# Token-order products with 512 weight columns at a time, and PSUM banks handled one token tile at a time

## The chip, the cores and the metric

The kernel runs on one core of a Trainium2 chip. The metric is device time in microseconds for one execution, as the median of several runs. The engines are named as the profile names them: PE (matrix products) with PEld (loading of the stationary operand), DVE, ACT, POOL, and SP, which issues most DMAs. Products land in PSUM, in tiles of 128x512 fp32 that are called banks here; DVE and ACT read them out.

## The reference

The program computes a two-layer trunk on 512 tokens of width 1024, all in fp32. Cut to what matters here:

```
for l in range(2):
    h = rmsnorm(x, norm_mix_g[l])
    a_q, a_k, a_v, a_gk, a_g, b_z, b_xbc, b_dt, c_q, c_k, c_v, gates = split(h @ w_in[l])
    y_gla  = gla_mixer(a_q, a_k, a_v, a_gk, a_g, ...)     # 4 heads, key 128, value 256, causal chunks
    y_ssm  = ssd_mixer(b_z, b_xbc, b_dt, ...)              # 4 groups of 8 heads
    y_diff = diff_mixer(c_q, c_k, c_v, positions, ...)     # 8 heads, two softmaxes of 64 each, value 128
    mixed  = sigmoid gates * (y_gla @ w_br_gla, y_ssm @ w_br_ssm, y_diff @ w_br_diff), summed
    x = x + mixed @ w_out[l]
    x = x + square(relu(rmsnorm(x) @ w_mlp_up[l])) @ w_mlp_down[l]
return rmsnorm(x)
```

`h @ w_in[l]` has 14,384 columns. Ten slices of 512 columns of it per layer matter here: `a_v` and `a_g` (GLA, 1024 columns each) and `c_q`, `c_k`, `c_v` (differential attention, 1024 columns each).

## The kernel before, in words

Every fp32 value that goes through a large product is split into a high part and a rest (both in the type fp32r), and a product is three: high times high, high times rest, rest times high. The activations stay in SBUF as pairs of `hl` tiles with the model dimension in the partitions. The weights come by DMA as blocks of 512 KB (`wraw`, 2 buffers); half a block at a time is split by ACT (`whi`) and by DVE or POOL (`wlo`), 4 buffers each. `Weight.split` (L511) does that.

There are two kinds of large ("dense") products. Most are in feature order: 128 weight columns are the stationary operand and 512 tokens stream, and the result takes one PSUM bank with features in the partitions (`item_a`, L848; `item_a2` does two such results, L876). The second kind is in token order, `item_b` (L924): 128 tokens of the activations are the stationary operand and **256 weight columns** stream, so that the result has tokens in its partitions. One item covers 256 columns and all 512 tokens: four token tiles share two banks, half a bank each. It takes both banks when it starts, runs 8 k-steps of 12 products of 128x256, and hands both to `fin` when the last one is issued. There are 20 such items per layer: GLA v and g for 4 heads (`gla_head`, `vg_item`, L1311), and q, k, v for 4 pairs of differential heads (`diff_pair`, `nat_item`, L1579).

PSUM has 4 banks under the name `d` for dense results and 4 under the name `m` for the small products of the mixers. A `d` bank is given back when its last reader is done: for v a copy by ACT and a subtraction by DVE (`z`, `tw`), for g a Tanh by ACT and a multiplication by DVE (`z`), for q, k, v of the attention one ACT copy.

The order of everything is made when the program is built. `Flow.run` keeps a clock of its own and a list of mixer tasks (Python generators, which yield what they wait for: an `Event`, or room in a pool) and of dense items. It issues a task's next step when what that waits for should be there, and otherwise a piece of the dense item that is running; another dense item is begun only when the running one has ended. The other engines' instructions are recorded by `Timed` and let out in order of their planned start (`Model.post`). So each engine has one fixed queue, and on the chip each instruction waits for the semaphores of what it needs: if DVE is later than planned, PE stands still at the first instruction that needs it, with everything behind.

Names: `z` (in the order listings `z4`) are tiles for gated and natural-order results, pool size 5; `tw` are tiles of the SSD decay weights and the v rests, pool size 3; `pj`, `tt`, `g1`, `hl` are further tiles of the mixers. `cth` is a two-buffer ring for scratch.

The two lines that take and fill a token-order result:

```
o = it.held[t // 2].ap[:, (t % 2) * 256:(t % 2) * 256 + 256]
f.mm(o, ah[:, ts], wh[:, j], k == 0 and t % 2 == 0, False)
```

The layer's items stand in this order in the list: SSD groups 0 to 3 (B, C, four X, four Z each, with the branch products `w_br_ssm` of the group before), then per GLA head K, Q, V, G with the last `w_br_ssm` after head 0 and eight gate items after head 1, then q, k, v of the four pairs, then gates, `w_br_gla`, `w_br_diff`, `w_out` and the MLP. The planner looks 16 items ahead and may take a later one.

## Time and profile before

| what | value |
|---|---|
| median of 3 runs | 2842.09 us (2841.82 to 2842.11) |
| span of the profiled execution, first to last instruction | 2836.2 us |
| PE busy in it | 2744.4 us, 97% |
| DVE busy | 1847.2 us, 65% |
| ACT busy | 1239.0 us, 44% |
| POOL busy | 774.7 us, 27% |
| mean granted clock of PE | 0.985 |

The page gives the profiled execution by its span; the median of the runs stands 5.9 us above that, which is what lies around the first and last instruction. The busy time of PE counts matmuls to the end of their way through the array, with overlap, so it says where PE stood still (the gaps) and not how long one product holds it; that is read from the distance between the starts of products that follow each other.

### The profile page before, as it was taken

To read this page: it belongs to the slowest core of one execution; us is meant where nothing else is said; L and a number is where in the kernel's file an instruction comes from. 1 tells how busy PE (TensorE), PEld (TensorE's weight loads), DVE (VectorE), ACT (ScalarE), POOL (GpSimd) and SP (SyncE) were. 2 spreads that over 40 slices of the span, in tenths; PEclk is the share of its full clock that TensorE was granted. 3 is DMA by queue.
4 is the path that set the end of the run, shared out by engine and by line. 5 is a ranking of instruction groups with operands and counts; after the bars stand their busy time and mean duration, and the time that the engine had idled before them with its cause. 6 is when DMAs were issued, how large, how long until landed. Compare 5 with 4: busy or idle time off the path is not lost.

```text
span 2836.2 us, 44502 instructions
## 1 busy us (share of the span) xinstructions
PE 2744.4 (97%) x16908; PEld 2349.9 (83%) x16908; DVE 1847.2 (65%) x3848; ACT 1239.0 (44%) x2381; POOL 774.7 (27%) x821
## 2 busy tenths in 40 slices
PE   7799999999999999999998999989999999999998
PEld 5678788899998888888866778878999988888887
DVE  7797878757777355444487888785666754654445
ACT  4355445545655333223344444454556543432222
POOL 4555454313232001001036343452223210011001
PEclk9899999999999999999999999999999999999999
DMA  4334432332222343333335343323222223333332
GB/s 133 92 107 110 113 112 76 85 86 78 69 68 75 97 126 94 96 95 100 95 95 138 93 119 101 110 61 94 81 81 63 75 82 102 116 100 98 96 98 83
DMA packets 458226, 268.97 MB, mean 95 GB/s; under 512 B 19014, under 2 KB 450748, under 8 KB 458012
## 3 DMA queue, kind: packets, MB, share of 16 engines
q1 hardware_dynamic: 457396, 265.07, 33.5%
q8 instruction: 133, 2.18, 0.3%
q10 hardware_dynamic: 616, 1.06, 0.1%
q14 instruction: 81, 0.66, 0.1%
HBM read 259.60 MB, written 6.49 MB: 94 GB/s over the span
## 4 chain that ended last, share of the span: by engine, by line
PE 82%; DVE 9%; POOL 2%; DMA 2%; issue 2%; ACT 2%; SPq 1%; DVEq 0%; ACTq 0%; POOLq 0%
PE d L353 73%; PE m L353 7%; PE m L357 2%; DVE tt L79 2%; DVE wlo L79 2%; DVE pj L79 1%; POOL tw L79 1%; DMA tw<-acs 1%; DVE g L79 1%; SPq L79 1%; DVE hl L79 1%; DVE z L79 1%; DMA wraw<-in_w_in 0%; ACT tt L79 0%; ACT whi L79 0%
## 5 line engine op out<-in xcount | busy, mean ns | idle before, releaser
L353 PE MATMUL d<-hl,whi 128*128 128x512 f32 (+2 forms) x5696 | 1779.3, 394 | 32.8 <-DVE tt L79 13.4
L353 PEld LDWEIGHTS d<-hl,whi 128*128 128x128 f32 (+1 forms) x5696 | 1059.5, 189 | 250.3 <-issue 24.4
L353 PE MATMUL d<-hl,wlo 128*128 128x512 f32 (+2 forms) x2848 | 1114.2, 391 | 7.9 <-DVE wlo L79 7.3
L79 ACT ACTIVATE whi<-wraw 128x512 fp32r<-128x512 f32 (+1 forms) x868 | 544.1, 628 | 1099.0 <-PE d L353 954.3
L79 DVE TENSOR_TENSOR wlo<-wraw,whi 128x512 fp32r<-128x512 f32 (+1 forms) x762 | 578.5, 762 | 483.8 <-ACT whi L79 477.7
L353 PEld LDWEIGHTS d<-hl,wlo 128*128 128x128 f32 (+1 forms) x2848 | 537.7, 189 | 123.7 <-DVE wlo L79 8.5
L353 PE MATMUL d<-whi,hl 128*128 128x256 f32 x2560 | 482.0, 289 | 0.0
L353 PEld LDWEIGHTS d<-whi,hl 128*128 128x128 f32 x2560 | 401.8, 193 | 2.9
L353 PE MATMUL d<-wlo,hl 128*128 128x256 f32 x1280 | 363.5, 284 | 0.0
L79 POOL TENSOR_TENSOR wlo<-wraw,whi 128x512 fp32r<-128x512 f32 x106 | 147.1, 1390 | 725.7 <-ACT whi L79 451.1
L79 POOL TENSOR_TENSOR tt<-tt 128x512 f32<-128x512 f32 (+1 forms) x132 | 151.6, 1158 | 625.9 <-ACT hl L79 530.2
L353 PEld LDWEIGHTS d<-wlo,hl 128*128 128x128 f32 x1280 | 246.3, 192 | 0.0
L79 DVE TENSOR_TENSOR res<-res,d 128x512 f32<-128x512 f32 (+1 forms) x130 | 86.7, 676 | 135.7 <-PE d L353 133.8
L79 POOL TENSOR_SCALAR tw<-tw,acn 128x128 f32<-128x128 f32 x101 | 92.1, 927 | 70.4 <-DMA tw<-acs 61.6
L79 ACT ACTIVATE tt<-tt 128x256 f32<-128x256 f32 (+3 forms) x190 | 87.6, 502 | 30.8 <-DMA tt<-acs 14.0
L79 DVE SCALAR_TENSOR_TENSOR pj<-d,cols,pj 128x511 f32<-128x511 f32 (+2 forms) x120 | 88.7, 743 | 1.5 <-ACT pj L79 0.3
L79 POOL TENSOR_TENSOR tw<-tw,tt 128x1024 f32<-128x1024 f32 x32 | 82.2, 2579 | 14.5 <-ACT tw L79 14.2
L79 ACT ACTIVATE tt<-m 128x512 f32<-128x512 f32 (+6 forms) x133 | 59.3, 451 | 54.7 <-PE m L353 34.2
L79 ACT ACTIVATE pj<-m 64x256 fp32r<-64x256 f32 (+1 forms) x160 | 66.7, 421 | 35.9 <-PE m L357 21.4
L353 PE MATMUL m<-z,tt 128*128 128x128 f32 (+1 forms) x432 | 75.2, 284 | 3.1 <-DVE g L79 1.7
L79 ACT ACTIVATE tw<-m,mx 128x384 f32<-128x384 f32 (+3 forms) x128 | 66.8, 524 | 25.4 <-DVE mx L79 24.3
L79 DVE SCALAR_TENSOR_TENSOR tt<-d,tt 128x512 f32<-128x512 f32 x64 | 44.0, 690 | 51.3 <-PE d L353 49.9
(179 smaller groups left out, 2621.9 us busy)
## 6 DMA issues: line engine op xcount, KB each, us to landing
wraw<-in_w_in SPq DMA_DIRECT2D x224, 512.0 KB
wraw<-in_w_mlp_up SPq DMA_DIRECT2D x64, 512.0 KB
wraw<-in_w_mlp_down SPq DMA_DIRECT2D x64, 512.0 KB
tw<-acs SPq DMA_DIRECT2D x32, 512.0 KB
wraw<-in_w_br_ssm SPq DMA_DIRECT2D x32, 512.0 KB
wraw<-in_w_br_gla SPq DMA_DIRECT2D x16, 512.0 KB
wraw<-in_w_br_diff SPq DMA_DIRECT2D x16, 512.0 KB
wraw<-in_w_out SPq DMA_DIRECT2D x16, 512.0 KB
```

What stands on the lines that cost most here:

```text
L79: fn = lambda a=args, k=kw: real(*a, **k)
L353: self.model.post(self.clock - c, lambda: self.nc.tensor.matmul(out, lhsT, rhs, start=start, stop=stop))
L357: self.model.post(self.clock - 0.109, lambda: self.nc.tensor.transpose(out, in_, ident))
```

## The change

`item_b` is replaced by `item_w`. One item now covers 512 columns of weights: a weight half-block is 128 rows of the model dimension by 512 columns (before: 256 rows by 256 columns), a k-step is 12 products of 128x512, and there are 8 half-blocks. Each of the four token tiles has a bank of its own. The bank for tile t is taken just before that tile's first products, and after the last k-step `fin` is called for each tile as soon as its products are issued, so banks go back one at a time. Per layer there are 10 such items in place of 20.

So that 512 columns belong together, the mixers work on more heads at a time: `gla_duo` has the V and G items of two heads in common and lists K, Q of both heads ahead of them; `diff_duo` has q, k, v of four heads (before: two). The results are cut into `z` tiles by token pairs instead of by head, the v rests move from `tw` to `z`, and the pool `z4` has 8 tiles instead of 5. `rope` works on two token tiles and eight half-heads instead of four and four: as many elements and calls as before. In the listing of the layer the last `w_br_ssm` items and the eight gate items both come after the first GLA duo. `rs_y` has 6 buffers instead of 2, and `dynamic_dma_scratch_size=1024` reserves less SBUF, which makes room for the larger pool; SP and ACT issue the DMAs as before.

```
-    def item_b(self, w, c0, acts, fin, extra=(), cond=()):
+    def item_w(self, w, c0, acts, fin, extra=(), cond=()):
         def body(it, i, wt):
-            wh, wl = wt
-            for j in range(2):
-                k = i * 2 + j
-                ...
-                for t in range(NT):
-                    o = it.held[t // 2].ap[:, (t % 2) * 256:(t % 2) * 256 + 256]
-                    ts = slice(t * P, (t + 1) * P)
-                    f.mm(o, ah[:, ts], wh[:, j], k == 0 and t % 2 == 0, False)
-                    f.mm(o, al[:, ts], wh[:, j], False, False)
-                    f.mm(o, ah[:, ts], wl[:, j], False, k == KT - 1 and t % 2 == 1)
-        blocks = [b for h in range(2) for b in Block(self, [w[h * 512:(h + 1) * 512, c0:c0 + 256]], 4, 256).parts()]
-        return self.item(blocks, [("d", ([P, 512],))] * 2 + list(extra), body, fin, acts, cond, False)
+            wh, wl = [v[:, 0] for v in wt]
+            ...
+            for t in range(NT):
+                if i == 0:
+                    yield {"d": 1}
+                    it.banks.append(self.T("d"))
+                else:
+                    yield None
+                o = it.banks[t].ap
+                ts = slice(t * P, (t + 1) * P)
+                f.mm(o, ah[:, ts], wh, i == 0, False)
+                f.mm(o, al[:, ts], wh, False, False)
+                f.mm(o, ah[:, ts], wl, False, i == KT - 1)
+                if i == KT - 1:
+                    fin(it, t, it.banks[t])
+        blocks = [b for k in range(0, KT, 2)
+                  for b in Block(self, [w[k * P:(k + 2) * P, c0:c0 + S]], 2, S).parts()]
+        return self.item(blocks, list(extra), body, lambda it: None, acts, cond, False)
...
+    def gla_duo(self, l, duo, h, slot, evy):
+        ...
+        for hd in (2 * duo, 2 * duo + 1):
+            self.gla_head(l, hd, h, shared, slot, evy[hd])
+        ...
+            def fin(it, t, ps):
+                x = it.held[t // 2].ap[:, t % 2]
+                if gate:
+                    self.act(x, ps.ap, AF.Tanh, scale=0.5)
+                    V.scalar_tensor_tensor(x, x, 1.0, ps.ap, op0=ALU.add, op1=ALU.mult)
+                    ...
+                else:
+                    self.split(x, it.held[2 + t // 2].ap[:, t % 2], ps.ap)
+                ps.free()
...
+        vg_item(O_V + duo * 512, False)
+        vg_item(O_G + duo * 512, True)
...
+    def diff_duo(self, l, duo, h, slot, evy):
...
+            def fin(it, t, ps):
+                x = it.held[t // 2]
+                self.act(x.ap[:, t % 2], ps.ap, AF.Copy)
+                ps.free()
+                if t % 2 and i < 2:
+                    self.rope(x.ap, t - 1)
...
-        for hd in range(4):
-            self.gla_head(l, hd, h, gs[hd // 2], evg[hd])
-            if hd == 0:
+        for duo in range(2):
+            self.gla_duo(l, duo, h, gs[duo], evg)
+            if duo == 0:
                 self.ssm_part(l, 3, evy[3], quads, merged, evm[3])
-            if hd == 1:
                 self.ssm_gates(l, h, merged, evm[3], gated)
-        for pr in range(4):
-            self.diff_pair(l, pr, h, ds[pr // 2], evd[pr // 2])
+        for duo in range(2):
+            self.diff_duo(l, duo, h, ds[duo], evd[duo])
```

The order on the engines changes with it. First place: PE in layer 0 where the first V item begins, behind the last Z item of the SSD mixer (`d_3270` before, `d_3310` after). Each name is one bank's worth of result. Before:

```order
L353 MATMUL d_3270<-hl_371,wlo_3233 128x512
L353 MATMUL d_3326<-whi_3268,hl_369 128x256
L353 MATMUL d_3326<-whi_3268,hl_370 128x256
L353 MATMUL d_3326<-wlo_3269,hl_369 128x256
L353 MATMUL d_3326<-whi_3268,hl_369 128x256
L353 MATMUL d_3326<-whi_3268,hl_370 128x256
L353 MATMUL d_3326<-wlo_3269,hl_369 128x256
L353 MATMUL d_3327<-whi_3268,hl_369 128x256
```

After:

```order
L353 MATMUL d_3310<-hl_371,wlo_3273 128x512
L353 MATMUL d_3366<-whi_3308,hl_369 128x512
L353 MATMUL d_3366<-whi_3308,hl_370 128x512
L353 MATMUL d_3366<-wlo_3309,hl_369 128x512
L353 MATMUL d_3373<-whi_3308,hl_369 128x512
L353 MATMUL d_3373<-whi_3308,hl_370 128x512
L353 MATMUL d_3373<-wlo_3309,hl_369 128x512
L353 MATMUL d_3382<-whi_3308,hl_369 128x512
L353 MATMUL d_3382<-whi_3308,hl_370 128x512
L353 MATMUL d_3382<-wlo_3309,hl_369 128x512
L353 MATMUL d_3444<-whi_3308,hl_369 128x512
```

Two banks carried the whole V item; now the first k-step alone goes into four, the fourth (`d_3444`) after nine products.

The same place on DVE. `z4_...<-z4_...,d_...` is the last read of a Z item's bank; the `pj` and `hl` rows between belong to the end of SSD group 2, the `wlo` rows split weights. Before:

```order
L79 SCALAR_TENSOR_TENSOR pj_2389<-pj_2389,cols0_92,tt_3240 128x512
L79 TENSOR_TENSOR wlo_3405<-wraw_3300,whi_3404 128x512
L79 TENSOR_TENSOR hl_3278<-pj_2389,hl_3277 128x512
L79 TENSOR_TENSOR wlo_3439<-wraw_3352,whi_3438 128x512
L79 SCALAR_TENSOR_TENSOR z4_3071<-z4_3071,d_3270 128x512
L79 TENSOR_TENSOR wlo_3472<-wraw_3352,whi_3471 128x512
L79 TENSOR_TENSOR tw_3135<-d_3326,z4_3134 128x512
L79 TENSOR_TENSOR tw_3135<-d_3327,z4_3134 128x512
```

After:

```order
L79 SCALAR_TENSOR_TENSOR z4_2311<-z4_2311,d_3246 128x512
L79 TENSOR_TENSOR wlo_3365<-wraw_3274,whi_3364 128x512
L79 SCALAR_TENSOR_TENSOR pj_2161<-pj_2161,cols0_92,tt_3280 128x512
L79 TENSOR_TENSOR hl_3318<-pj_2161,hl_3317 128x512
L79 SCALAR_TENSOR_TENSOR pj_2207<-pj_2207,cols0_92,tt_3280 128x512
L79 SCALAR_TENSOR_TENSOR pj_2251<-pj_2251,cols0_92,tt_3280 128x512
L79 TENSOR_TENSOR hl_3318<-pj_2207,hl_3317 128x512
L79 TENSOR_TENSOR hl_3318<-pj_2251,hl_3317 128x512
L79 SCALAR_TENSOR_TENSOR pj_2428<-pj_2428,cols0_92,tt_3280 128x512
L79 TENSOR_TENSOR wlo_3448<-wraw_3274,whi_3447 128x512
L79 TENSOR_TENSOR hl_3318<-pj_2428,hl_3317 128x512
L79 SCALAR_TENSOR_TENSOR z4_2376<-z4_2376,d_3310 128x512
```

In both orders the last Z item's bank is read out at the end of that chain; before, the V item's own banks follow it and nothing on PE needed that bank earlier.

Second place: DVE in layer 1, again where the first V item begins (the Z items' banks are `d_16884`, `d_16948` before and `d_15926`, `d_15991` after). Before:

```order
L79 SCALAR_TENSOR_TENSOR z4_16703<-z4_16703,d_16884 128x512
L79 SCALAR_TENSOR_TENSOR pj_15846<-pj_15846,cols1_93,tt_16917 128x512
L79 TENSOR_TENSOR wlo_17000<-wraw_16911,whi_16999 128x512
L79 TENSOR_TENSOR hl_16945<-pj_15846,hl_16944 128x512
L79 SCALAR_TENSOR_TENSOR z4_16764<-z4_16764,d_16948 128x512
```

After:

```order
L79 TENSOR_SCALAR tw_15934<-tw_15934,acn_13540 128x128 x6
L79 SCALAR_TENSOR_TENSOR z4_15743<-z4_15743,d_15926 128x512
L79 SCALAR_TENSOR_TENSOR pj_14886<-pj_14886,cols1_93,tt_15960 128x512
L79 TENSOR_TENSOR wlo_16043<-wraw_15954,whi_16042 128x512
L79 SCALAR_TENSOR_TENSOR z4_15804<-z4_15804,d_15991 128x512
```

Six `tw` rows of a third SSD chunk moved ahead of the two reads, and the `hl` row moved behind the second.

## Rows read from the trace of the kernel before

**Rows 1.** The page, part 1 and a line of part 2 (tenths busy, 40 slices)

```profile
PE 2744.4 (97%) x16908; PEld 2349.9 (83%) x16908; DVE 1847.2 (65%) x3848; ACT 1239.0 (44%) x2381; POOL 774.7 (27%) x821
...
PE   7799999999999999999998999989999999999998
```

**Rows 2.** Waits of PE over the span: total us, times, longest

```profile
PE m L353 <- DVE tt L79: 14.6, 12, 3.5
...
PE d L353 <- DVE pj L79: 11.8, 2, 8.8
```

**Rows 3.** Groups by form: busy us, mean ns of one | idle before

```profile
L353 PE MATMUL d<-whi,hl 128*128 128x256 f32 x2560 | 482.0, 289 | 0.0
...
L353 PE MATMUL d<-wlo,hl 128*128 128x256 f32 x1280 | 363.5, 284 | 0.0
```

**Rows 4.** Chain that ended last: start us, us, what, products

```profile
692.34 8.63 PE d L353 x72
...
1089.96 339.64 PE d L353 x1497
```

**Rows 5.** PE timeline, end of a Z item and start of V, layer 0

```profile
365.14 0.39 PE L353 MATMUL d<-hl,wlo 128*128 128x512 f32 x1
365.37 0.40 PE L353 MATMUL d<-whi,hl 128*128 128x256 f32 x2
```

**Rows 6.** DVE timeline at the same place

```profile
367.11 0.68 DVE L79 SCALAR_TENSOR_TENSOR z<-z,d 128x512 f32<-128x512 f32 x1
367.70 0.74 DVE L79 SCALAR_TENSOR_TENSOR pj<-pj,cols,tt 128x512 f32<-128x512 f32 x1
368.88 2.48 DVE L79 TENSOR_TENSOR wlo<-wraw,whi 128x512 fp32r<-128x512 f32 x1 [0.43 <-ACT whi L79]
...
377.85 0.68 DVE L79 SCALAR_TENSOR_TENSOR z<-z,d 128x512 f32<-128x512 f32 x1
```

**Rows 7.** PE timeline, start of the first V item of layer 1

```profile
1753.06 0.40 PE L353 MATMUL d<-whi,hl 128*128 128x256 f32 x2
```

**Rows 8.** DVE timeline at the same place

```profile
1753.99 0.68 DVE L79 SCALAR_TENSOR_TENSOR z<-z,d 128x512 f32<-128x512 f32 x1
...
1758.18 1.77 DVE L79 TENSOR_TENSOR hl<-pj,hl 128x512 fp32r<-128x512 f32 x1
1759.88 0.68 DVE L79 SCALAR_TENSOR_TENSOR z<-z,d 128x512 f32<-128x512 f32 x1
```

**Rows 9.** PE timeline, the longest wait in GLA of layer 0

```profile
469.62 0.66 PE L353 MATMUL m<-tt 128*32 128x32 f32 x32 [4.01 <-DVE sd L79]
```

**Rows 10.** Stretches: busy us of each engine, then PE's granted clock, DMA

```profile
440.00:520.00 80.00, 73.19 (x721) 63.74 (x720) 71.42 (x155) 45.45 (x101) 42.13 (x34) 0.94 0.24 71
469.60:476.00 6.40, 6.38 (x151) 6.05 (x152) 5.81 (x14) 1.56 (x5) 3.52 (x3) 0.59 0.25 84
680.00:760.00 80.00, 80.00 (x661) 79.20 (x660) 55.55 (x151) 49.60 (x121) 22.13 (x38) 1.00 0.26 73
1683.00:1690.00 7.00, 6.97 (x39) 5.58 (x39) 5.57 (x9) 2.79 (x5) 1.84 (x2) 0.76 0.63 188
1825.00:1905.00 80.00, 71.53 (x765) 61.55 (x764) 69.56 (x152) 44.99 (x100) 36.71 (x31) 0.94 0.24 71
```

**Rows 11.** PE timeline, last products of a G item

```profile
613.15 0.28 PE L353 MATMUL d<-wlo,hl 128*128 128x256 f32 x1
```

**Rows 12.** DVE timeline: that G item's two banks read out

```profile
614.63 1.28 DVE L79 SCALAR_TENSOR_TENSOR z<-z,d 128x512 f32<-128x512 f32 x2
```

**Rows 13.** PE timeline, last product of an attention item

```profile
696.36 0.28 PE L353 MATMUL d<-wlo,hl 128*128 128x256 f32 x1
```

**Rows 14.** ACT timeline: that item's two banks read out

```profile
698.08 0.60 ACT L79 ACTIVATE z<-d 128x512 f32<-128x512 f32 x1
...
700.94 0.60 ACT L79 ACTIVATE z<-d 128x512 f32<-128x512 f32 x1
```

More of the change, by code (lines that the diff above doesn't have):

```diff
@@ L963, in rsqrt_small @@
         v = pool.tile([P, n], F32, name="rs_v", bufs=2)
-        y = pool.tile([P, n], F32, name="rs_y", bufs=2)
+        y = pool.tile([P, n], F32, name="rs_y", bufs=6)
         t = pool.tile([P, n], F32, name="rs_t", bufs=2)
@@ L1309, in gla_head @@
         qk_item(O_Q + hd * P, "q", st["evq"], P ** -0.5)
-        def vg_item(c0, key, ev, gate):
-            def fin(it):
-                x = it.held[2]
-                for i in range(2):
-                    ps = it.held[i]
-                    pv = ps.ap.rearrange("p (t c) -> p t c", c=256)
-                    xv = x.ap[:, 2 * i:2 * i + 2]
-                    if gate:
-                        self.act(xv, pv, AF.Tanh, scale=0.5)
-                        V.scalar_tensor_tensor(xv, xv, 1.0, pv, op0=ALU.add, op1=ALU.mult)
-                        G.tensor_tensor(xv, xv, self.gnr.unsqueeze(1).broadcast_to([P, 2, 256]), op=ALU.mult)
-                        ps.free()
-                    else:
-                        self.split(xv, it.held[3].ap[:, 2 * i:2 * i + 2], pv)
-                        ps.free()
-                st[key] = x if gate else it.held[2:]
-                ev.t = f.at(*[x.ap for x in it.held[2:]])
-            self.item_b(w, c0, h, fin, extra=[("z4", ([P, NT, 256],))] if gate else
-                        [("z4", ([P, NT, 256], F32R)), ("tw", ([P, NT, 256], F32R))])
-        vg_item(O_V + hd * 256, "v", st["evv"], False)
-        vg_item(O_G + hd * 256, "g", st["evg"], True)
         def gates():
@@ L1503, in scores @@
             qe.free()
-            for x in parts + st["v"]:
+            for x in parts + shared["v"]:
                 x.free()
@@ L1533, in finish @@
             if done[0] == NT:
-                st["g"].free()
+                for x in shared["g"]:
+                    x.free()
                 evy.t = f.at(*[q.ap[:, m0:m0 + 2] for q in slot[0]])
@@ L1556, in diff_lambda, with rope @@
         nc.vector.tensor_scalar(self.dcol, self.cols[l][:, C_DN:C_DN + 1], 1.0 - li, None, op0=ALU.mult)
-    def rope(self, x):
+    def rope(self, x, t0):
         G = self.nc.gpsimd
@@ L1576, in diff_pair @@
         nat, evs = [None] * 3, [Event() for _ in range(3)]
-        left = [2]
+        left = [4]
         half = (slice(0, 64), slice(64, P))
         def nat_item(i, off):
-            def fin(it):
-                x = it.held[2]
-                for j in range(2):
-                    self.act(x.ap[:, 2 * j:2 * j + 2], it.held[j].ap.rearrange("p (t c) -> p t c", c=256), AF.Copy)
-                    it.held[j].free()
-                if i < 2:
-                    self.rope(x.ap)
-                nat[i] = x
-                evs[i].t = f.at(x.ap)
-            self.item_b(w, off + pr * 256, h, fin, extra=[("z4", ([P, NT, 256],))])
+            def fin(it, t, ps):
[4 more added lines that the diff above has]
+                    self.rope(x.ap, t - 1)
+                if t == NT - 1:
+                    for b in it.held:
+                        b.users = 1 if i == 2 else 4
+                    nat[i] = it.held
+                    evs[i].t = f.at(*[b.ap for b in it.held])
+            self.item_w(w, off + duo * S, h, fin, extra=[("z4", ([P, 2, S],))] * 2)
         for i, off in enumerate((O_CQ, O_CK, O_CV)):
             nat_item(i, off)
+        nat_of = lambda i, t, hh: nat[i][t // 2].ap[:, t % 2, hh * P:(hh + 1) * P]
         def head(hh):
-            hd = pr * 2 + hh
             def turn(i, t0, n):
@@ L1598, in turn @@
                 for t in range(n):
-                    f.tr(tp.ap[:, t * P:(t + 1) * P], nat[i].ap[:, t0 + t, hh * P:(hh + 1) * P], self.ident)
-                if hh == 1 and t0 + n == NT:
-                    nat[i].free()
+                    f.tr(tp.ap[:, t * P:(t + 1) * P], nat_of(i, t0 + t, hh), self.ident)
+                for b in nat[i][t0 // 2:(t0 + n) // 2]:
+                    b.free()
                 return tp
@@ L1700, in step @@
             if left[0] == 0:
-                nat[2].free()
+                for b in nat[2]:
+                    b.free()
             V.tensor_scalar(o.ap[:, t], op.ap[:, :P], rc[:, t, 0:1], None, op0=ALU.mult)
@@ L1704, in step @@
             ev.t = f.at(o.ap[:, t])
-        for hh in range(2):
+        for hh in range(4):
             f.spawn(head(hh))
```

51 lines of the change are left out of this document (35 added, 16 removed).

## The prediction, made before the change was run

> **What bounds the kernel now.** I read the page's busy times first, then who makes PE wait, then the stretches. PE is busy 2744.4 of 2836.2 us, and the slices show it near full from the third of 40 on [rows 1]. The reader is to see two things: PE is the bound wherever it stands at 9, and the 92 us without it lie in a few places where PE waits for DVE [rows 2]. In the attention part PE is busy 80.00 of 80 us; in the GLA part it is 73.19 of 80 in layer 0 and 71.53 of 80 in layer 1, with DVE busy 71.42 and 69.56 of the same 80 [rows 10]. So in the first place time saved on PE is time saved, in the second DVE sets the pace, and a saving on PE may only become more waiting.
>
> **What the wider products save.** The 3840 narrow products (2560 and 1280) [rows 3] run in 40 items. Their spacing is read from the chain: 72 of them in 8.63 us, 119.9 ns each; 1497 products of 512 columns take 339.64 us, 226.9 ns each [rows 4]. Two narrow ones cost 239.8 ns, one wide one 226.9, so 12.9 ns go for each pair. 3840 / 2 = 1920 pairs give 1920 x 12.9 ns = **24.7 us less on PE**. All else that items do is equal in number: bytes of weights, weight splits (half as many items, twice as many halves), read-outs of 128x512, `rope` and gate multiplications. I cost those at nothing; they lie beside PE's work and their count per microsecond of PE hardly moves. The larger `z4` pool lets some Z items of SSD groups 2 and 3 in layer 0 go earlier; layer 1 keeps its order up to the first V item. I cost that at nothing too, with 3 us to either side.
>
> Here the Trainium skill speaks against the change. Its page "TensorE: Matmul & The Clock Gate", section "Back-to-back issue gap", gives for products alone a spacing of N/2.4 ns plus 2.5 ns at full clock, which would leave 2.5 ns a pair, an estimated 4.8 us in all. The trace's 119.9 and 226.9 ns do not agree with it: both are about 13 ns over their columns.
>
> **What four banks cost: the first V item.** An item took two of the four `d` banks; now it takes all four within its first nine products, 9 x 0.2269 = 2.04 us. Whatever item came last must be read out by then, or PE stands, and with it every mixer product and weight behind it in PE's queue.
>
> Layer 0. Before, the first V item starts at 365.37, right behind a Z item [rows 5]. That Z item's bank is read last by the DVE multiplication at 377.85, which ends at 378.53 [rows 6]: DVE has the end of SSD group 2 in front of it. Nobody on PE waited, since V had two other banks. In the new order the fourth bank is that of the last Z item, and the same chain stands ahead of its read-out: from one `z` row to the next the old order takes 367.11 to 378.53 = 11.42 us [rows 6], with four weight splits in it; the new one has two, so 11.42 - 2 x 0.68 = 10.1 us. It begins 367.11 - 365.37 = 1.74 us after the V item's start, or up to 1.7 us later, since six `tw` rows (some 0.28 each) stand ahead. So the bank is free 11.8 to 13.5 us after the start and wanted after 2.04: PE waits 9.8 to 11.5 us. If the one stretched row (2.48 us for a split, where 0.68 is usual) is ordinary this time, it is 1.8 less, 8.0. I take **10 us**.
>
> Layer 1. V starts at 1753.06 [rows 7], the two Z read-outs begin at 1753.99 and 1759.88 [rows 8], the second ends at 1760.56, 7.50 us after the start. In the new order the `hl` row of 1.77 us stands behind it, and six `tw` rows (1.7 us) ahead: 5.7 to 7.4 us, less 2.04 = 3.7 to 5.4. I take **4.5 us**.
>
> A long wait has a second price. After the 4.01 us wait [rows 9] the granted clock of the next 6.4 us is 0.59, so part of them ran at 1.2 instead of 2.4 GHz: 6.4 x 0.41 = 2.6 us lost; behind the wait of 11.8 - 8.8 = 3.0 us in layer 1 [rows 2] it is 7.0 x 0.24 = 1.7 us [rows 10]. I add 2.6 and 1.7.
>
> **What four banks cost elsewhere.** Other places per layer where a wide item starts or ends tight: the first G item, the two-bank `w_br_ssm` products after it, the second G item, the first attention item right behind it, and the first and second items of the second attention duo. Ten to twelve in all; I count 11. A bank is given back 2.04 us before the same tile of a following wide item needs it. A G item's two banks are read out by 614.63 + 1.28 = 615.91, its last product began at 613.15 [rows 11, 12]: about 2.5 us after its end, 0.5 us over the cover. In attention, where ACT is full of exponentials, the second bank is free at 700.94 + 0.60 = 701.54, some 4.9 us after the end of the product begun at 696.36 [rows 13, 14], 2.9 us over. An item between, or small products of the tasks, cover all of it. Between 0 and 2.9 a place I take 0.5, nearest to the G row: 11 x 0.5 = **5.5 us**, with 0 and 15 as ends. Where a bank is late, nothing new is waiting on DVE or ACT; their queues only drain.
>
> **The GLA part.** Two heads' score stages now run in the same stretch, under one G item and four `w_br_ssm` items, where before they came one after the other. PE's idle time there is 80 - 73.19 = 6.8 and 80 - 71.53 = 8.5 us [rows 10], because DVE is late. The DVE work is the same, denser at first and thinner behind. I carry over the 15.3 us unchanged: 0 in the sum, -8 and +20 as bounds.
>
> The Trainium skill, "Trainium Kernel Development and Optimization", section "Best Practices", says that tiling for TensorE speeds up compute but not the evacuation of PSUM. The rows on the banks above agree with it.
>
> **Sum**, on the profiled span of 2836.2 us: -24.7 + 10 + 2.6 + 4.5 + 1.7 + 5.5 + 0 = -0.4 us. The runs stand 5.9 us over the span, which nothing here touches, so the time is 2842.1 - 0.4 = 2841.7; I say **2841 us**.
>
> **The rivals.**
> Faster: DVE is less late. The waits at V take their low ends (8.0 and 3.7, less clock loss, 3), the others 1, and PE's standing early lets DVE catch up, so half of the 15.3 us in GLA goes: -24.7 + 8 + 3.7 + 3 + 1 - 7.6 = -16.6, **2825 us**. For it: in attention PE never waits and DVE is busy only 55.55 of 80 [rows 10]. Against it: the chain of rows 6 does not depend on PE, and between V and GLA lie 70 us in which DVE would recover anyway.
> Slower: DVE cannot carry two GLA heads at once. If PE's idle time there doubles (+15.3) the sum is +14.9, **2857 us**. It decides where the two heads' stretch has over 12 us of PE idle a layer; from there the change loses. For it: DVE is already at 89% of such a stretch. Against it: the stretch behind is thin, and PE's products of the other head can fill.
> The change doesn't do what it says: the 13 ns are not a price per product but something that wide products with moving weights keep. Then nothing is saved and the waits stay: +24.3, **2866 us**. Against it: the spacing of rows 4 is constant over 1497 products. By the skill's formula above, read as such a case, it would be 2842.1 - 4.8 + 24.3, an estimated 2862 us.
>
> **How the numbers follow.** The forecast (own range 2834 to 2848) has 0.38, the faster rival 0.34, the slower one 0.24, no saving 0.04. About 0.2%, 5.7 us, is what a measurement of this kernel can tell from no change. Of the forecast's share 0.34 lie within that and 0.02 on either side: faster 0.36, same 0.34, slower 0.30. The range of 8 in 10 reaches from the faster rival to the slower one, 2824 to 2859.
>
> **What would show it.** Wide products with moving weights at 227 ns and 1920 of them; one PE wait of 8 to 12 us on DVE `z` at the first V item of layer 0 and one of 4 to 5 in layer 1; waits under 1 us at the other starts; 13 to 17 us of PE idle in GLA. The forecast is wrong if the V waits are under 5 us together, if the GLA idle time is under 8 or over 30, or if the spacing is not 227 ns.

## The result, and the profile after

The changed kernel takes 2858.8 us (median of 4 executions, 2858.0 to 2863.6), the kernel before 2841.95 (4 executions, 2836.8 to 2842.1). The ratio of these executions on record is 1.0071, 95% interval 1.0054 to 1.0089, so the change makes the kernel slower by some 20 us. (The two medians alone are 16.9 us apart; in the comparisons of the experiments the kernel before has medians of 2837.2 to 2838.3.) The forecast of 2841 us, 0.4 us less than before, stood for no change that can be measured, and was wrong: the kernel is slower beyond the interval. The time itself lies at the upper end of the range, near the 2857 of the slower rival, though not for that rival's reason.

The page of the changed kernel, part 1 and a line of part 2, and two of its groups (busy us, mean ns of one | idle before and its releaser):

```profile
PE 2742.2 (96%) x14988; PEld 2245.1 (78%) x14988; DVE 1874.5 (65%) x3835; ACT 1240.2 (43%) x2381; POOL 794.1 (28%) x834
...
PE   7799989999999999999997999999999999999998
...
L353 PE MATMUL d<-whi,hl 128*128 128x512 f32 x1280 | 412.2, 404 | 20.1 <-DVE z L79 19.6
...
L353 PE MATMUL d<-wlo,hl 128*128 128x512 f32 x640 | 253.1, 395 | 0.0
```

The 1920 wide products are there in place of the 3840 of [rows 3]. PE's busy time has hardly moved, the span has grown to 2861.9, and 19.6 us of idle time stand ahead of the wide products, put down to DVE's `z` rows. The waits of PE to be read beside [rows 2] (total us, times, longest):

```profile
PE m L353 <- DVE tt L79: 20.9, 18, 2.8
PE d L353 <- DVE z L79: 19.6, 6, 10.9
PE d L353 <- DVE pj L79: 13.2, 2, 10.1
```

From the chain that ended last (start us, us, what, products), the spacing of the wide products in attention is 42.87 us / 189 = 226.8 ns each.

```profile
2098.94 42.87 PE d L353 x189
```

The PE timeline where the first V item starts, layer 0 and then layer 1, to be read beside [rows 5, 7]. The item begins at 376.51, as 375.83 is the last Z item's:

```profile
375.83 0.61 PE L353 MATMUL d<-hl,whi 128*128 128x512 f32 x2
...
376.51 0.61 PE L353 MATMUL d<-whi,hl 128*128 128x512 f32 x2
...
379.35 0.74 PE L353 MATMUL d<-whi,hl 128*128 128x512 f32 x2 [1.32 <-DVE z L79]
...
391.21 1.22 PE L353 MATMUL d<-whi,hl 128*128 128x512 f32 x2 [10.88 <-DVE z L79]
...
1781.95 0.74 PE L353 MATMUL d<-whi,hl 128*128 128x512 f32 x2 [1.54 <-DVE z L79]
...
1787.67 1.22 PE L353 MATMUL d<-whi,hl 128*128 128x512 f32 x2 [4.74 <-DVE z L79]
```

In both layers PE stands for the third and then for the fourth bank. By the distance between the starts of products, which also counts what a product in flight hides, these are 1.5 + 11.1 = 12.5 us in layer 0 and 1.7 + 4.9 = 6.6 us in layer 1.

**Where the 25.7 us between the two profiled spans lie.** The profiled execution of the changed kernel is its slowest, some 5 us above its other three, so these 25.7 us stand for some 21 in the times. I add up, over all consecutive products of each trace, the distance between their starts less the steady distance (227 ns for 512 columns, 175 for 384, 120 for 256); products of fewer columns count with their whole distance. That is the time lost in each stage, here as the difference to the kernel before. The cut between GLA and attention is made where two fifths of a layer's token-order columns are done, so that where an order interleaves the two, their sum is meant. The experiments of the next section stand in the same table, all in us.

| kernel | products | SSD 0 | GLA 0 | attention, MLP 0 | SSD 1 | GLA 1 | attention 1 to end | sum of all |
|---|---|---|---|---|---|---|---|---|
| before_again | 0 | +0.7 | -0.3 | +0.1 | +1.6 | -0.1 | 0 | +1.9 |
| **after** | -25.0 | +6.8 | +23.1 | +6.1 | +3.4 | +6.5 | +5.6 | +26.5 |
| pairs | 0 | +3.8 | +22.0 | +3.7 | +0.1 | +5.5 | +3.6 | +38.7 |
| v_narrow | -22.5 | +3.9 | +5.8 | +5.5 | +1.8 | -2.0 | +5.5 | -2.1 |
| duo0_narrow | -20.0 | +6.1 | -8.9 | +20.0 | +1.9 | -6.3 | +23.7 | +16.4 |
| z_hold | -25.0 | +2.0 | +26.6 | +5.4 | +4.5 | +6.5 | +5.7 | +25.7 |
| duo0_z_hold | -20.0 | -1.0 | +2.9 | +22.2 | +2.0 | -7.4 | +21.8 | +20.5 |
| z_copy | -25.0 | +10.2 | +12.5 | +5.4 | -0.7 | +9.9 | +5.6 | +18.1 |
| pools | 0 | +5.3 | +7.2 | +3.8 | +1.7 | 0 | +5.0 | +23.0 |
| pools_hold | 0 | +0.7 | +0.9 | 0 | +0.5 | -0.2 | -0.1 | +1.9 |
| before_slack | 0 | +4.3 | +5.3 | -0.8 | -3.7 | -6.5 | +0.5 | -0.8 |
| before_lag | 0 | +14.9 | -2.0 | -0.8 | +4.7 | +0.8 | -2.0 | +15.7 |
| after_slack | -25.0 | +9.5 | +12.3 | +21.0 | -5.8 | +11.3 | +22.4 | +45.7 |
| after_lag | -25.0 | +7.0 | +16.3 | +20.4 | +7.8 | +5.6 | +22.6 | +54.8 |
| gla_wide | -10.0 | +5.2 | +22.8 | +0.7 | +1.8 | +5.2 | +0.6 | +26.2 |
| attn_hold | -15.0 | +0.3 | -1.2 | +5.4 | +3.5 | 0 | +5.3 | -1.7 |
| attn_hold, once more | -15.0 | +0.6 | +2.9 | +5.4 | -0.2 | 0 | +5.4 | -0.7 |
| mix | -20.0 | +1.3 | +1.4 | +7.1 | +4.4 | -1.0 | +7.1 | +0.4 |
| no_mask_mult | -25.0 | -16.2 | +17.3 | +5.4 | -10.8 | -1.8 | +5.3 | -25.8 |

The saving of the forecast is there within 0.3 us, and twice as much is lost: 19.1 us at the two V items, the rest in pieces of a few us over every stage but the MLP. One execution of a kernel differs from the next by some 4 us in a stage (the two rows of attn_hold, in GLA 0 and SSD 1), so single entries below that mean nothing.

### The profile page after: what moved, and what is told of

It is laid out like the page before. It is cut to its first block, busy times and chain, and to the rows that moved or that the text cites. A ratio compares the mean times of both kernels' runs of the same rounds, so it can differ in the third digit from the quotient of the medians.

```text
span 2861.9 us, 40688 instructions
## 1 busy us (share of the span) xinstructions
PE 2742.2 (96%) x14988; PEld 2245.1 (78%) x14988; DVE 1874.5 (65%) x3835; ACT 1240.2 (43%) x2381; POOL 794.1 (28%) x834
## 5 line engine op out<-in xcount | busy, mean ns | idle before, releaser
L79 DVE TENSOR_TENSOR wlo<-wraw,whi 128x512 fp32r<-128x512 f32 (+1 forms) x746 | 562.9, 757 | 495.6 <-ACT whi L79 473.6
L353 PE MATMUL d<-whi,hl 128*128 128x512 f32 x1280 | 412.2, 404 | 20.1 <-DVE z L79 19.6
L79 POOL TENSOR_TENSOR wlo<-wraw,whi 128x512 fp32r<-128x512 f32 x122 | 169.5, 1393 | 691.8 <-ACT whi L79 362.4
L79 POOL TENSOR_TENSOR tt<-tt 128x512 f32<-128x512 f32 x133 | 153.0, 1161 | 633.2 <-ACT hl L79 530.2
L353 PEld LDWEIGHTS d<-whi,hl 128*128 128x128 f32 x1280 | 235.1, 191 | 68.3 <-DVE z L79 22.1
L353 PE MATMUL d<-wlo,hl 128*128 128x512 f32 x640 | 253.1, 395 | 0.0
L353 PEld LDWEIGHTS d<-wlo,hl 128*128 128x128 f32 x640 | 121.9, 190 | 26.8
L79 DVE TENSOR_TENSOR tt<-tt,pj 128x256 f32<-128x256 f32 (+1 forms) x112 | 83.5, 788 | 4.4 <-ACT tt L79 4.3
L353 PEld LDWEIGHTS m<-z,tt 128*128 128x128 f32 x488 | 69.0, 190 | 14.8 <-issue 4.3
```

What stands on the lines that cost most here:

```text
L79: fn = lambda a=args, k=kw: real(*a, **k)
L353: self.model.post(self.clock - c, lambda: self.nc.tensor.matmul(out, lhsT, rhs, start=start, stop=stop))
```

## The experiments

The theories: A, the wide items lose their gain in waits for banks behind DVE. B, the gain itself is not real. C, the larger pool makes another order, and that order costs. D, DVE is late by a fixed amount, and PE meets that lateness at one place or another. Later ones are named where they come in. Ratios are to the kernel before, run beside each.

### The price of a product: pairs

```
-                f.mm(o, ah[:, ts], wh, i == 0, False)
-                f.mm(o, al[:, ts], wh, False, False)
-                f.mm(o, ah[:, ts], wl, False, i == KT - 1)
+                for x, y, z, e in ((ah, wh, i == 0, False), (al, wh, False, False), (ah, wl, False, i == KT - 1)):
+                    f.mm(o[:, :256], x[:, ts], y[:, :256], z, False)
+                    f.mm(o[:, 256:], x[:, ts], y[:, 256:], False, e)
```

> The changed kernel with each of its 1920 products of 128x512 made as two of 128x256, side by side in the same bank; all else is in nearly the same order, and banks are taken and given back as in the changed kernel. Theory A (the price per product is real, and the change loses its 24.7 us again in waits): the wide products' saving is undone, 1920 x 12.9 ns = 24.7 us more than the changed kernel's 2858.8, less a few us because PE comes later to the banks it waits for: 2883, between 2876 and 2887. Theory B (the 13 ns are not a price per product): no change, 2857 to 2861.

Measured: 2876.4 us, 1.0138 (1.0116 to 1.0161). Against the changed kernel's 1.0071 that is 0.67%, or 19 us more. In the traces the products take 25.0 us more by the steady distances, and 12.8 us less are lost, half of that in the SSD part, where both kernels have nearly the same order and executions differ. The V wait stays what it was, so it belongs to the four banks and not to the width of the products:

```profile
389.06 0.58 PE L353 MATMUL d<-whi,hl 128*128 128x256 f32 x1 [10.89 <-DVE z L79]
```

So B is out: a second product of half the width costs 13 ns by the spacing in the traces, and 10 by the times (19 us over 1920 products, with 8 us to either side).

### Where the waits go: v_narrow, duo0_narrow, z_copy

v_narrow makes V of the first two heads by two items of two banks; duo0_narrow makes their G so as well.

```
+        if duo == 0:
+            v_half(0)
+            v_half(1)
+        else:
+            vg_item(O_V + duo * 512, False)
```

> The changed kernel, except that V of the first two GLA heads of each layer is made by two items of 256 columns with two banks each, as before the change; 18 of 20 wide items stay. The order up to there is that of the changed kernel. Theory A (the first V item's wait for its fourth bank is the largest loss): the waits of 12.5 and 6.6 us and the low clock behind them (some 3.8) go, and 2 x 96 pairs x 12.9 ns = 2.5 us come back: 2858.8 - 22.9 + 2.5 = 2838, between 2834 and 2844. Theory D (PE only runs into the same late DVE at the next place): half or less of that, 2848 to 2858.

Measured: 2837.75 us, 0.9998 (0.9987 to 1.0009). The wait at V is gone and with it the whole loss. The time is in the range of A and outside that of D, but the trace is not so simple. Part of the wait has moved on, to the G item behind: its third bank is one of the V item before it, and DVE, busy with the end of the last SSD group, reads that only at 474.87:

```profile
475.70 0.77 PE L353 MATMUL d<-whi,hl 128*128 128x512 f32 x1 [10.22 <-DVE z L79]
...
1866.67 0.76 PE L353 MATMUL d<-whi,hl 128*128 128x512 f32 x1 [4.07 <-DVE z L79]
```

```profile
471.71 1.32 DVE L79 TENSOR_TENSOR hl<-pj,hl 128x512 fp32r<-128x512 f32 x1
472.95 0.68 DVE L79 TENSOR_TENSOR wlo<-wraw,whi 128x512 fp32r<-128x512 f32 x1
473.56 1.39 DVE L79 TENSOR_TENSOR tt<-tt,pj 128x256 f32<-128x256 f32 x2
474.87 1.27 DVE L79 TENSOR_TENSOR z<-d,z 128x512 fp32r<-128x512 f32 x2
```

> The kernel v_narrow with G of the first two heads made by two items of 256 columns too; the second GLA duo and all of the attention stay wide (16 of 20 wide items). In v_narrow PE waits 10.2 us (layer 0) and 4.1 us (layer 1) for a bank of the first G item. Theory A (each wide item that starts behind a late DVE waits for its third and fourth bank): these waits go and 2.5 us of product time come back, 2 of clock go: 1.0000 - 13.8 / 2838 = 0.995, between 0.993 and 0.997 of the kernel before. Theory D (PE only meets the same lateness at the next place): 0.998 to 1.002.

Measured: 2850.2 us, 1.0039 (1.0024 to 1.0054), outside the ranges of A and D, and slower than v_narrow where A expected 14 us less. GLA and attention together lose 11.1 (layer 0) and 17.4 us (layer 1) more than in the kernel before; the big waits are gone and many small ones are there.

In z_copy the Z items of the last SSD group give their bank back without DVE:

```
 self.act(z, ps.ap, AF.Tanh, scale=0.5)
+if g == 3:
+    x = it.held[-1]
+    self.act(x.ap, ps.ap, AF.Copy)
+    ps.free()
+    V.scalar_tensor_tensor(z, z, 1.0, x.ap, op0=ALU.add, op1=ALU.mult)
...
```

> The changed kernel, in which the four Z items of the last SSD group give their bank back after a second ACT instruction that copies it to SBUF (a pj tile of its own), where before the multiplication on DVE was the last reader; the multiplication then reads the copy. All 20 items per two layers stay wide. Theory A (PE waits at the first V item only because DVE's queue holds the bank of a Z item): the waits of 12.5 and 6.6 us fall to under 3 together, and the low clock behind them goes: 2858.8 - 19 = 2840, 0.999 to 1.002 of the kernel before. Theory D (the same lateness meets PE at the next place): 1.004 to 1.008.

Measured: 2857.4 us, 1.0065 (1.0049 to 1.0082), in the range of D. By the starts the V waits are 4.1 us in layer 0 and 5.5 in layer 1, where A expected under 3 together; the longest are 2.42 us, and 2.46 and 2.75, all put down to DVE's `pj` rows. The order is another again (the extra tiles come from the pool of `pj`), and its SSD part loses 10.2 us, 5.11 at one place that had no such wait:

```profile
301.48 0.79 PE L353 MATMUL d<-hl,whi 128*128 128x512 f32 x1 [5.11 <-DVE res L79]
...
362.30 0.66 PE L353 MATMUL d<-whi,hl 128*128 128x512 f32 x1 [2.42 <-DVE pj L79]
```

So two of the three edits that took a wait away did not bring its length back, and each of them moved everything behind it. That made the order itself the suspect.

### The order alone: pools, pools_hold, z_hold, duo0_z_hold

The edit of pools, shortened to the three values that change:

```
-("z4", mx, 5)            name="rs_y", bufs=2
+("z4", mx, 8)            name="rs_y", bufs=6           dynamic_dma_scratch_size=1024
```

> The kernel before with the pools of the change alone: 8 z4 tiles for 5, 6 rs_y for 2, and the smaller DMA scratch. All products stay 128x256 and take two banks as before. The larger pool lets Z items go earlier and so moves the order of the SSD part. Theory A (the loss is in the four banks): no change within 3 us, 2839 to 2845. Theory C (a good part of the loss is the new order of the SSD part, where the trace of the changed kernel shows 6.8 us more before the first V item of layer 0): 2846 to 2852.

Measured: 2857.9 us, 1.0074 (1.0053 to 1.0095), more than C expected. With every product narrow and two banks to an item, the pools alone cost as much as the whole change. There is no wait at V; the loss is 5.3 us in SSD 0, 7.2 in GLA 0 and 3.8 and 5.0 around the two attentions. Two of its waits that the kernel before has not:

```profile
464.07 0.77 PE L353 MATMUL m<-tt,one_row 128*128 128x512 f32 x1 [4.42 <-DVE tt L79]
...
920.86 0.50 PE L353 MATMUL d<-hl,whi 128*128 128x512 f32 x1 [1.91 <-ACT whi L79]
```

pools_hold keeps these pools, but items that take a `z4` tile leave three free (`need["z4"] = 4`, and 7 in place of 4 for the norm), so that the planner has the old cap.

> The kernel pools (before, with 8 z4 tiles, 6 rs_y and the smaller DMA scratch), in which every item that takes a z4 tile leaves 3 free, so that the planner has the old cap of 5 and PE the order of the kernel before, but for a few rows. Theory C (the 21 us that pools lost come from the order alone): within 0.15% of the kernel before. Theory G (the smaller DMA scratch or the pool itself costs on the chip): 1.003 to 1.008.

Measured: 2839.1 us, 1.0007 (0.9998 to 1.0017), and no stage loses 1 us. C is shown for the kernel before, and G is out: neither the larger pool nor the smaller scratch costs anything that can be told from nothing (at most 0.17%); the order that the planner makes of them does.

z_hold puts the same rule on the Z items of the changed kernel, duo0_z_hold on those of duo0_narrow.

> The changed kernel, in which a Z item of the SSD part starts only when 4 of the 8 z4 tiles are free, so that Z items hold no more tiles than with the pool of 5. Up to the first V item of layer 0 PE then has the order of the kernel before; the wide items and their four banks stay. Theory C (the SSD part of layer 0 is slower because Z items went earlier): the 3 to 6 us of that stretch come back, the waits at V stay, 1.0050 to 1.0062 of the kernel before (the changed kernel has 1.0071). Theory A (only the four banks cost): no change, 1.0066 to 1.0076.

> Both edits together: Z items that leave 4 of 8 z4 tiles free, and V and G of the first two heads by narrow items. If A and C both hold and add up, 3 to 6 us less than duo0_narrow: 0.992 to 0.994 of the kernel before. If the place of the Z items does not matter: as duo0_narrow.

Measured: 1.0075 (1.006 to 1.009) for both, so neither is faster than the kernel it was made from: z_hold is in A's range and not in C's, and duo0_z_hold is slower than both of its expectations. In z_hold SSD 0 gets 4.8 us back (+2.0 for +6.8), as C says, but the time does not show it; the 3.5 us more in GLA 0 are within what two executions differ by. In duo0_z_hold there are 7 us less in SSD 0 and 14 more in GLA 0 and the attention behind it. Restoring one stage's order does not give its gain to the whole.

### Other orders of either kernel: before_slack, before_lag, after_slack, after_lag

```
-SLACK, LAG, BACK, AHEAD = 0.4, 0.15, 6.0, 16
+SLACK, LAG, BACK, AHEAD = 0.5, 0.15, 6.0, 16      (slack)
+SLACK, LAG, BACK, AHEAD = 0.4, 0.25, 6.0, 16      (lag)
```

> The kernel before with one constant of its planner moved (SLACK 0.5 for 0.4 us, the margin after which a task's next step is issued). No product, tile or bank changes, but the order on every engine is another. Theory E (any new order of this tuned kernel costs some 20 us of scattered waits, as the larger pools alone did): 2846 to 2862, 1.003 to 1.0085 of the kernel before. Theory F (orders are about equal, and what costs is particular to the larger pool): within 0.2%.

> The kernel before with another constant of its planner moved (LAG 0.25 for 0.15, the share by which waits are held to be longer than planned). Again the order alone changes. Theory E: 1.003 to 1.0085 of the kernel before. Theory F: within 0.2%.

> The changed kernel with SLACK 0.5 for 0.4: the same items, pools and banks in another order. Theory E (the order of the changed kernel is one draw among many, and its loss is partly this draw): anywhere from 0.997 to 1.008 of the kernel before, the first V item's wait anywhere from 0 to 15 us. Theory A (the loss belongs to the wide items): 1.005 to 1.008, with the wait at V between 8 and 15 us.

> The changed kernel with LAG 0.25 for 0.15: another order again. Theory E: anywhere from 0.997 to 1.008 of the kernel before; a longer margin makes the planner's events later, nearer to what DVE does on the chip, so rather the lower half. Theory A: 1.005 to 1.008, with the wait at V between 8 and 15 us.

Measured: before_slack 0.9999 (0.999 to 1.0009), before_lag 1.0071 (1.0055 to 1.0086), after_slack 1.0161 (1.0145 to 1.0176), after_lag 1.0192 (1.0173 to 1.021). E and F each got one of the first two: a new order of the kernel before costs between nothing and 20 us. The changed kernel, though, shows no sign of an unlucky draw: its two other orders are 25 and 34 us slower still, which no theory of mine had. Their V items wait 13.6 and 13.6 us (slack) and 6.0 and 7.9 us (lag, less than A's 8 in layer 0), and in and behind the attention of four heads they lose some 16 us a layer more than the changed kernel. Slack's two V waits of layer 0, and its longest wait behind the attention:

```profile
377.42 0.77 PE L353 MATMUL d<-whi,hl 128*128 128x512 f32 x1 [7.61 <-DVE pj L79]
...
384.50 0.79 PE L353 MATMUL d<-whi,hl 128*128 128x512 f32 x1 [5.45 <-DVE z L79]
...
990.88 0.45 PE L357 MATMUL m<-ident,tt 128*128 128x128 f32 x1 [5.34 <-DVE tt L79]
```

The wait at the first V item is in all four orders of the changed kernel's structure with Z read by DVE (after, z_hold, slack, lag): it belongs to the item that takes four banks, not to the draw.

### Which half loses: gla_wide, attn_hold, mix

gla_wide keeps `gla_duo` and takes the old `diff_pair`; attn_hold keeps `diff_duo` and takes the old `gla_head`, with the leave-three rule outside the attention.

```
+        for hd in range(4):
+            self.gla_one(l, hd, h, gs[hd // 2], evg[hd])
...
         for duo in range(2):
             self.diff_duo(l, duo, h, ds[duo], evd[duo])
```

> Wide items in GLA alone (8 of the 20), the attention by items of 256 columns for two heads at a time, the pools of the change. Up to the attention of layer 0 it is the changed kernel, wait at V included. Theory A (GLA's wide items lose, those of the attention gain 14.9 and lose 11): some 4 us more than the changed kernel, 1.007 to 1.010 of the kernel before. Theory H (the attention part loses too): less than the changed kernel, 1.002 to 1.006.

> Wide items in the attention alone (12 of the 20), GLA by items of 256 columns as before, and all users of z4 outside the attention leave 3 of 8 tiles free, so that the order is that of the kernel before up to the attention of layer 0. Products: 1152 pairs x 12.9 = 14.9 us less. If the attention loses 5.5 us a layer in waits, as in the changed kernel: 2838 - 14.9 + 11 = 2834, 0.9975 to 1.0005 of the kernel before (theory A: the loss is in GLA). Theory H (the attention of four heads at a time is itself a losing part, with the wait behind its last heads that two other orders show, 12 to 16 us a layer): 1.002 to 1.008.

Measured: gla_wide 1.0099 (1.0084 to 1.0114), attn_hold 0.9992 (0.9983 to 1.0001), both in the range of A. GLA's wide items bring 10.0 us and lose 28.0 in the two GLA stages; those of the attention bring 15.0 and lose 10.7 in the two attention stages (5.4 + 5.3), while GLA, whose products have the old order but for one, stays within what executions differ by. H, in the sense of a losing attention, is out for this order. The one new wait over 1 us there is that of the last wide item for its fourth bank:

```profile
820.17 0.50 PE L353 MATMUL d<-whi,hl 128*128 128x512 f32 x1 [1.34 <-DVE tt L79]
```

mix makes V and G of heads 2 and 3 wide as well, on top of attn_hold, which ran once more beside it.

> attn_hold with V and G of GLA heads 2 and 3 wide as well (16 of the 20 wide items), heads 0 and 1 one after the other by items of 256 columns. In the changed kernel the first and second item of the second GLA duo waited for no bank (0 and 0.1 us). Theory A (a wide item gains its 1.24 us wherever DVE is not late): 384 pairs x 12.9 = 5.0 us less than attn_hold, 2831, 0.996 to 0.9985 of the kernel before. Theory C (the new order from head 2 on costs as much as other new orders, 5 to 20 us): 0.9995 to 1.006.

> attn_hold once more, beside mix, for a narrower interval. It saves 14.9 us of product time and its trace shows some 5 us of new waits a layer in the attention: 0.9975 to 0.9995 of the kernel before. If it does not beat the kernel before: 0.9995 to 1.0005.

Measured: mix 0.9998 (0.9989 to 1.0007), attn_hold 0.9997 (0.9988 to 1.0007). The second duo's 5.0 us are not in the time, as C expected. No wide item of GLA waits more than 0.5 us for a bank in mix; of what is lost again, 3.5 us lie in the two attentions behind (7.1 each for attn_hold's 5.4), in an order that is new from there on. The two runs of attn_hold, -0.08% and -0.03%, show no gain beyond their scatter: no version here that does all of the work beats the kernel before.

### Why the chain at V is late: no_mask_mult

```
-            G.tensor_tensor(wa, wa, st["cb"].ap[:, c].unsqueeze(1).broadcast_to([P, 8, P]), op=ALU.mult)
+            cbv = st["cb"].ap[:, c].unsqueeze(1).broadcast_to([P, 8, P])
+            nc.step("G", "tensor_tensor", [wa], [wa, cbv], None)
```

> The changed kernel without the 32 multiplications of the SSD decay weights with the masked C-B products on POOL (tw<-tw,tt 128x1024, some 2.5 us each); the planner still counts them, so that every other instruction stands where it stood. This leaves out a part of the SSD mixer. In the trace of the changed kernel two DVE rows of the chain ahead of the first V item's fourth bank run while such a POOL row runs, in both layers: 2.44 and 2.82 us where 0.68 and 0.74 are usual (layer 0), 2.46 and 2.83 (layer 1), 3.8 to 3.9 us together. Theory P (a DVE row that meets a POOL row is held until that is done, and this is what makes the chain late): both rows at their usual length, the waits at V fall from 12.5 to 8.7 and from 6.6 to 2.7 us, 0.998 to 1.005 of the kernel before. Theory Q (the rows are long for another reason): rows and waits as they were, at most the few us that wait for these products themselves, 1.005 to 1.0075.

Measured: 2812.4 us, 0.991 (0.989 to 0.993), 46 us less than the changed kernel and below P's range. The products of PE have the changed kernel's order. The V waits are 7.2 and 1.4 us by the starts. The DVE timeline of the changed kernel (first fence), its POOL timeline (second), and DVE at the same place of no_mask_mult (third):

```profile
378.62 0.68 DVE L79 SCALAR_TENSOR_TENSOR z<-z,d 128x512 f32<-128x512 f32 x1
379.22 2.44 DVE L79 TENSOR_TENSOR wlo<-wraw,whi 128x512 fp32r<-128x512 f32 x1
381.59 2.82 DVE L79 SCALAR_TENSOR_TENSOR pj<-pj,cols,tt 128x512 f32<-128x512 f32 x1
...
390.48 0.68 DVE L79 SCALAR_TENSOR_TENSOR z<-z,d 128x512 f32<-128x512 f32 x1
```

```profile
378.75 5.11 POOL L79 TENSOR_TENSOR tw<-tw,tt 128x1024 f32<-128x1024 f32 x2 [0.89 <-ACT tw L79]
```

```profile
353.97 0.68 DVE L79 SCALAR_TENSOR_TENSOR z<-z,d 128x512 f32<-128x512 f32 x1
354.57 0.68 DVE L79 TENSOR_TENSOR wlo<-wraw,whi 128x512 fp32r<-128x512 f32 x1
355.17 0.74 DVE L79 SCALAR_TENSOR_TENSOR pj<-pj,cols,tt 128x512 f32<-128x512 f32 x1
...
361.98 0.68 DVE L79 SCALAR_TENSOR_TENSOR z<-z,d 128x512 f32<-128x512 f32 x1
```

The two POOL rows end at 381.11 and 383.86; each of the two long DVE rows begins while one of them runs and ends about half a microsecond behind it. Without the POOL rows they take 0.68 and 0.74. From the first `z` row to the end of the second it is 12.5 us with the POOL rows and 8.7 without, the 3.8 that was expected. P is shown at this place; the wait for the third bank (1.5 and 1.7 us) has gone as well. Of the 46 us as a whole, a part is not lengthened DVE rows but POOL's own 80 us and the products that waited for them; this run does not part the two.

### The kernel before, once more: before_again

> The kernel before once more, unchanged, for its second profile and the time beside the span of every execution. If the 5.9 us by which the runs stood over the profiled span are fixed, each execution shows them; if the profiled execution was itself a short one, time less span is the 1.7 us that the changed kernel shows in all four executions, and spans lie between 2835 and 2841.

Measured: 1.0006 (0.9995 to 1.0017). In each of its ten executions the time is 1.7 us over the span. So is it in the four of the changed kernel.

## Why the prediction was wrong, point by point

- **The saving** was right. 24.7 us were forecast, 25.0 are in the trace, with 226.8 ns a product; pairs shows it as a price per product. The spacing that the Trainium skill gives for products alone in "TensorE: Matmul & The Clock Gate", section "Back-to-back issue gap", would have left 4.8 us, an estimate from its 2.5 ns; the 19 us that pairs costs in time, with 8 to either side, speak against it here.
- **The first V items** were right in mechanism, place and releaser, and too small: 12.5 and 6.6 us for 10 and 4.5. What failed is the count of the chain ahead of the bank. It carried over the one stretched row that the order before has in each layer (2.48 us in [rows 6]; 2.49 in layer 1, first line below). In the new order two POOL multiplications stand back to back there and two rows are stretched, by 3.8 us together: in layer 0 as shown under no_mask_mult, in layer 1 as in the POOL and DVE rows of the changed kernel below. In layer 0 no_mask_mult shows the POOL rows to be the cause; the layer 1 waits fell with them too.

```profile
1755.77 2.49 DVE L79 TENSOR_TENSOR wlo<-wraw,whi 128x512 fp32r<-128x512 f32 x1 [0.43 <-ACT whi L79]
```

```profile
1781.34 5.13 POOL L79 TENSOR_TENSOR tw<-tw,tt 128x1024 f32<-128x1024 f32 x2 [2.56 <-ACT tw L79]
```

```profile
1781.81 2.46 DVE L79 SCALAR_TENSOR_TENSOR pj<-pj,cols,tt 128x512 f32<-128x512 f32 x1
1784.19 2.83 DVE L79 TENSOR_TENSOR wlo<-wraw,whi 128x512 fp32r<-128x512 f32 x1
```

- **The low clock behind these waits** was priced at 4.3 us and cost 4.8. The 6.8 us after 391.2 ran at 0.63 of the clock and the 6.4 after 1787.6 at 0.64, so part of each ran at 1.2 instead of 2.4 GHz: 6.8 x 0.37 = 2.5 and 6.4 x 0.36 = 2.3 us (the clock is the third number from the end).

```profile
391.20:398.00 6.80, 6.79 (x20) 5.36 (x21) 0.93 (x2) 1.26 (x2) 0.00 (x0) 0.63 0.22 71
...
1787.60:1794.00 6.40, 6.33 (x18) 5.05 (x19) 5.23 (x7) 2.34 (x5) 2.02 (x2) 0.64 0.30 84
```

- **The other bank starts** were priced at 5.5 us and cost 2.1: 0.7 at the first attention item of either layer, 0.7 at the first G item of layer 1, under 0.1 at the start of each other wide item.
- **GLA's idle time**, carried over at 15.3 us, was right: over the stretches 440 to 560 and 1845 to 1965 PE is idle for 9.3 + 5.8 = 15.1. The slower rival, which came nearest in time, said that it would double; it did not, so its near hit is luck.

```profile
440.00:560.00 120.00, 110.68 (x944) 87.37 (x943) 106.75 (x242) 61.56 (x135) 62.23 (x58) 0.94 0.25 73
1845.00:1965.00 120.00, 114.18 (x957) 90.01 (x956) 107.07 (x255) 64.72 (x141) 51.58 (x47) 0.99 0.26 76
```

- **The larger pool, "at nothing" with "3 us to either side"**, is the step that failed and made the sign wrong. The pools alone, with narrow items, are 20 us slower (pools), and they cost nothing that can be measured where the order is held (pools_hold). The prediction weighed only the Z items that go earlier, with one bound for them; what the new order does to the stages behind, GLA 0 and the attentions, where most of the loss of pools lies, had no term at all.
- **The attention, "PE never waits"**, was costed only by its bank starts. It loses 6.1 and 5.6 us, 0.7 of each at a start. The largest others are PE's waits for the heads' own chain, now four heads long, 1.7 us in layer 0 as below; the rest of that layer is in pieces under 0.3 us, whose cause stays open:

```profile
809.70 0.46 PE L353 MATMUL m<-z,tt 128*128 128x128 f32 x2 [1.11 <-DVE pj L79]
...
927.06 0.35 PE L353 MATMUL m<-z,tt 128*128 128x128 f32 x1 [0.58 <-DVE pj L79]
```

- **The 5.9 us over the span** are not what lies around the first and last instruction: that is 1.7 us each time. The 5.9 came from setting a median of 2842.1 beside the span of another execution; the executions of that kernel, over all comparisons, run from 2830 to 2846, and its medians there lie 4 us under the 2842.1 that the forecast started from.

With all priced terms at their measured size the sum is -25.0 + 19.1 (V) + 4.8 (clock) + 2.1 (other starts) = +1.0, near the forecast of -0.4 partly by luck: V was 4.6 us too small and the other starts 3.4 too large. The 25.5 us that remain to the +26.5 of the table (some 5 of them belong to this one execution) stand in no term of the prediction: 10.2 in the SSD stages, 5.0 in GLA, 10.3 in attention. They lie in the new order and in the larger units of work, and how much belongs to which stays open. pools loses 23.0 us by order with two heads at a time, attn_hold 10.7 in attention with four heads and nearly the old order ahead of it, and in the changed kernel the two do not simply add. The V waits weigh about as much as this remainder: v_narrow, which takes them away, is level with the kernel before. No run has the larger units with narrow two-bank items throughout, which would part them.

## What to carry to other kernels

- A pool size or an item size that feeds a planner is an edit of the order of everything behind it. Price it by a run that changes the pool alone, and by one that holds the order with the new pool; in this kernel another order cost up to 20 us, as much as the whole change did.
- An item that takes all accumulator banks waits for the slowest reader of any of them. Follow the queue of the engine that reads the bank given back last, and price its rows as they are in that stretch, beside what runs on the other engines there.

## What the runs showed of the hardware

In the trace of the changed kernel 143 DVE rows are more than 0.8 us longer than the median of their kind, 162 us in all (113 rows and 126 us before; the changed kernel has 19 us more POOL time). 141 of the 143 began while a POOL row ran, and each time it was a TENSOR_TENSOR; of the 292 DVE rows that began beside another kind of POOL row none is long. None of the 143 reads a bank: of 1135 DVE rows with an input in PSUM 307 began beside a POOL row and none is long. Of the 742 `wlo<-wraw,whi` rows of 128x512, 128 began beside a POOL row and 30 are long. The Trainium skill's "GPSIMD Engine Reference", section "1. Specifications", says that POOL shares its SBUF interfaces with the vector engine, with contention for DVE instructions that have two SBUF inputs, among others. The long rows at V, with two tiles in SBUF each, agree with it. The trace shows the size: where a TENSOR_TENSOR of POOL still had more than half a microsecond to go beyond the usual end of a DVE row with two tiles in SBUF, 84 of 90 such rows ended no sooner than it. Leaving out 32 POOL rows of 2.5 us shortened the time by 46 us, the two profiled spans by 52.6, and DVE's busy time by 50.8:

```profile
PE 2726.4 (97%) x14988; PEld 2237.1 (80%) x14988; DVE 1823.7 (65%) x3835; ACT 1240.8 (44%) x2381; POOL 708.4 (25%) x802
```

Whether the mask multiplication can be had elsewhere for less (on DVE 128x1024 elements, or folded into another step) was not tried, nor whether leaving it out helps the kernel before.
